# SwiGLU gate and up as a Strassen product of 2x2 blocks, the down product woven between

## The chip, the cores and the metric

One core of one Trainium2 chip runs the whole program. The metric is the device time of one execution in microseconds (us), the median over several executions. The engines are named as the profile names them: PE is TensorE (matrix products, with PEld its weight loads), DVE is VectorE, ACT is ScalarE, POOL is GpSimd, and SP is SyncE, which issues the loads.

## The reference

The program computes a trunk of four layers on 512 frames of width 1024 in float32. Each layer has a mixer (pattern A, B, C, A) and a SwiGLU block; a final RMSNorm ends it.

```python
for i in range(DEPTH):
    hn = rmsnorm(x, norm1_g[i])
    ...
    x = x + y
    x = x + swiglu(rmsnorm(x, norm2_g[i]), ffn_w_gu[i], ffn_w_down[i])
return rmsnorm(x, final_g)

def swiglu(h, w_gu, w_down):
    g, u = jnp.split(h @ w_gu, 2, axis=-1)
    return (jax.nn.silu(g) * u) @ w_down
```

The SwiGLU's inner width is 2816, that is 22 tiles of 128. Only the four SwiGLU blocks are changed.

## The kernel before, in words

Everything is kept with features on the 128 partitions and the 512 frames on the free axis. `X[0..7]` are the eight 128 x 512 tiles of the residual. A float32 operand is split in two parts that TensorE takes at its fast float32r rate: `split` (L125 to L127) makes the high part by a cast on ACT and the low part by a subtraction on DVE. A product of two split operands takes three matmuls, high by high, high by low and low by high (`mm3`, L131 to L133). `dense` (L135) runs `mm3` over the k tiles into one PSUM bank. `weights` (L119) takes a tile of 128 x 1024 weights: it loads 512 KB into `raw` (three buffers) and splits it into `wH` and `wL` (four buffers each).

The norm is applied late. `norm_k` (L226) scales a finished `X[k]` by the norm's weight, and splits it (`hidden_k`, L234: `hH` on ACT at L246, `hL` on DVE at L247), and adds its square to `ssum`. The factor 1/rms per frame comes from `rms_cols` (a column per block of 128 frames, `rcol`) and `rms_rows` (the same along the free axis, `self.r`), and multiplies the products behind the matmuls.

`swiglu` (L301) goes over the 22 inner tiles in groups of 8, 8 and 6. For each tile it takes the gate's weights and the up's weights, each 8 k tiles by 128 outputs, as the stationary operand, with the frames moving, 24 matmuls of 128x512 for each of the two. DVE multiplies both banks by 1/rms (L320, L324), ACT takes the silu (L322), DVE multiplies (L325), and the result is split into `mH`, `mL`. After a group, the down product goes over the 8 output tiles: one tile of weights, 3 matmuls for each inner tile of the group, and `add_x` (L220) adds the bank to `X[m]` on DVE.

Nothing is ordered by a planner: each engine runs its instructions in the order that the tile framework's scheduler gave them when the program was built, and it waits only on semaphores. SP issues all loads, in one order too. A buffer that is taken again makes the instruction that writes it wait for the last reader of what it held.

Of the kernel before, what the change touches and what calls it, by code (L numbers as in the profile page):

```python
# [20 lines left out]
NB = 4  # L21
AH = 16
BH = 8
FT = 22
FGROUPS = ((0, 8), (8, 8), (16, 6))
CW = 2048
CT = 16
EPS = 1e-6
# [3 lines left out]
C_G1, C_G2, C_GF = 0, 32, 64  # L32
# [6 lines left out]
class Trunk:  # L39
# [194 lines left out]
    def hidden_k(self, k):  # L234
        nc = self.nc
        if k == 0:
            self.h_next = []
        g = self.vec[:, self.next_g + k:self.next_g + k + 1]
        if self.next_g == C_GF:
            y = self.hp.tile([P, S], F32, name=self.nm("y"), tag=f"hH{k}")  # L240
            nc.scalar.activation(out=y, in_=self.X[k], func=AF.Identity, scale=g)
            self.h_next.append(y)
        else:
            hi = self.hp.tile([P, S], F32R, name=self.nm("hH"), tag=f"hH{k}")
            lo = self.hp.tile([P, S], F32R, name=self.nm("hL"), tag=f"hL{k}")
            nc.scalar.activation(out=hi, in_=self.X[k], func=AF.Identity, scale=g)  # L246
            nc.vector.scalar_tensor_tensor(out=lo, in0=self.X[k], scalar=g, in1=hi.bitcast(F32),  # L247
                                           op0=ALU.mult, op1=ALU.subtract)
            self.h_next.append((hi, lo))

    def squares_k(self, k, pool=None):

# [45 lines left out]
        return pr  # L298


    def swiglu(self, l):  # L301
        nc = self.nc
        with ExitStack() as es:
            fp = es.enter_context(self.tc.tile_pool(name="ffn", bufs=2, side="right",
                                                    reuse_waits="tile"))
            for k0, kn in FGROUPS:
                acts = []
                for j in range(k0, k0 + kn):
                    gh, gl = self.weights(self.a["w_g"][l, j])
                    pg = self.acc()  # L310
                    self.dense(pg, gh, gl, self.h)
                    if j == 0:
                        self.rms_cols()
                    uh, ul = self.weights(self.a["w_u"][l, j])
                    pu = self.acc()
                    self.dense(pu, uh, ul, self.h)
                    if j == 0:
                        self.rms_rows()
                    g = fp.tile([P, S], F32, name=self.nm("g"), tag="g")
                    nc.vector.tensor_tensor(out=g, in0=pg, in1=self.r, op=ALU.mult)  # L320
                    sg = fp.tile([P, S], F32, name=self.nm("sg"), tag="sg")
                    nc.scalar.activation(out=sg, in_=g, func=AF.Silu)  # L322
                    u = fp.tile([P, S], F32, name=self.nm("u"), tag="u")
                    nc.vector.tensor_tensor(out=u, in0=pu, in1=self.r, op=ALU.mult)  # L324
                    nc.vector.tensor_tensor(out=u, in0=u, in1=sg, op=ALU.mult)  # L325
                    hi, lo = self.part_tiles()
                    self.split(u, hi, lo)
                    acts.append((hi, lo))
                for m in range(KT):
                    dh, dl = self.weights(self.a["w_d"][l, m, :, k0 * P:(k0 + kn) * P], kn * P)  # L330
                    pd = self.acc()
                    self.dense(pd, dh, dl, acts)
                    self.add_x(m, pd, k0 + kn == FT)


    def token_major(self, src, then=None):
# [662 lines left out]
def layouts(i):  # L999

    g = {k: np.asarray(v) for k, v in i.items()}
    c = np.ascontiguousarray

    def stat(w):
        K, M = w.shape
        return c(w.reshape(K // P, P, M // P, P).transpose(2, 1, 0, 3)).reshape(M // P, P, K)
# [9 lines left out]
    def outw(w):  # L1016
        n = w.shape[0] // S
        return c(w.reshape(n, 4, P, 4, 2, P).transpose(0, 3, 2, 4, 1, 5)).reshape(n, 4, P, 1024)

    def cols(v):  # L1020
# [34 lines left out]
        "w_g": np.stack([stat(w[:, :FT * P]) for w in g["ffn_w_gu"]]),  # L1055
        "w_u": np.stack([stat(w[:, FT * P:]) for w in g["ffn_w_gu"]]),
        "w_d": np.stack([stat(w) for w in g["ffn_w_down"]]),
    }


# [14 lines left out]
```

## Time and profile before

| what | value |
|---|---|
| median of 3 runs | 2528.62 us (2526.58 to 2528.68) |
| the profiled execution's own time | 2527.86 us |
| its span, from first to last instruction | 2526.2 us |
| mean granted TensorE clock | 0.996 |
| PE busy | 2498.8 us, 99% |
| DVE busy | 1382.9 us, 55% |
| ACT busy | 1065.9 us, 42% |
| POOL busy | 228.0 us, 9% |
| DMA | 89 GB/s mean over the span |

The share of busy time of PE is that of matmuls that overlap in the pipeline, so how many run one after another is read from their start times. The four SwiGLU blocks lie at about 266 to 630, 901 to 1267, 1544 to 1908 and 2153 to 2509 us of the span.

### The profile page before, as it was taken

How to read it: one execution, taken by the hardware profiler on the slowest of the kernel's cores; microseconds unless marked ns; L12 is line 12 of the kernel's file. 1: busy time of each engine (PE TensorE's matmuls, PEld its weight loads, DVE VectorE, ACT ScalarE, POOL GpSimd, SP SyncE). 2: the span in 40 equal slices, each digit the busy share in tenths (PEclk: the TensorE clock that was granted, in tenths of full speed). 3: DMA queues.
4: the chain of work that ended last, by engine and by line, in shares of the span. 5: the costliest groups of instructions: out<-in, count | busy, mean ns of one | idle time of the engine just before them, and what ended most of it. 6: DMA issues, size and time to landing. Idle time of an engine off the chain costs nothing.

```text
span 2526.2 us, 31856 instructions
## 1 busy us (share of the span) xinstructions
PE 2498.8 (99%) x12156; PEld 2098.5 (83%) x12156; DVE 1382.9 (55%) x2202; ACT 1065.9 (42%) x1779; POOL 228.0 (9%) x369
## 2 busy tenths in 40 slices
PE   8999999999999999999999999999999999999998
PEld 7898888888888888888888888888888888888886
DVE  7777444445777754444537655434456777444443
ACT  7776322223766642222433324222236776322222
POOL 2222100001000110000100001000011222000001
PEclk9999999999999999999999999999999999999998
DMA  4112232323122223232322222323232222232321
GB/s 145 60 60 76 99 93 100 93 95 103 62 76 84 92 92 99 93 101 91 101 92 91 93 84 100 93 99 98 94 93 76 69 68 76 92 98 94 101 88 62
DMA packets 69416, 226.00 MB, mean 89 GB/s; under 512 B 11793, under 2 KB 12817, under 8 KB 69265
## 3 DMA queue, kind: packets, MB, share of 16 engines
q1 hardware_dynamic: 69264, 223.98, 27.2%
q8 instruction: 96, 1.57, 0.3%
q14 instruction: 56, 0.45, 0.1%
HBM read 221.55 MB, written 2.10 MB: 89 GB/s over the span
## 4 chain that ended last, share of the span: by engine, by line
PE 95%; ACT 2%; DVE 2%; issue 1%; POOL 0%; DMA 0%; SPq 0%; DVEq 0%; POOLq 0%; ACTq 0%
PE acc L131 26%; PE acc L133 26%; PE acc L132 26%; PE acc L171 2%; PE acc L173 2%; PE acc L172 2%; PE pt L524 1%; PE acc L350 1%; PE acc L351 1%; PE acc L352 1%; PE po L539 1%; PE s L502 1%; PE s L501 1%; PE po L538 1%; PE ps L927 0%
## 5 line engine op out<-in xcount | busy, mean ns | idle before, releaser
L126 ACT CAST wH<-raw 128x1024 fp32r<-128x1024 f32 (+2 forms) x427 | 438.7, 1028 | 1118.1 <-PE acc L132 969.7
L131 PE MATMUL acc<-hH,wH 128*128 128x512 f32 x1984 | 783.2, 395 | 0.0
L133 PE MATMUL acc<-hH,wL 128*128 128x512 f32 x1984 | 773.9, 390 | 0.0
L132 PE MATMUL acc<-hL,wH 128*128 128x512 f32 x1984 | 773.2, 390 | 0.0
L127 DVE TENSOR_TENSOR wL<-raw,wH 128x1024 fp32r<-128x1024 f32 (+2 forms) x427 | 510.1, 1195 | 118.1 <-ACT wH L126 96.5
L133 PEld LDWEIGHTS acc<-hH,wL 128*128 128x128 f32 x1984 | 372.4, 188 | 78.7
L131 PEld LDWEIGHTS acc<-hH,wH 128*128 128x128 f32 x1984 | 372.8, 188 | 72.8 <-issue 0.5
L132 PEld LDWEIGHTS acc<-hL,wH 128*128 128x128 f32 x1984 | 373.1, 188 | 72.0 <-issue 0.2
L131 PE MATMUL acc<-mH,wH 128*128 128x512 f32 x1024 | 402.2, 394 | 0.2
L132 PE MATMUL acc<-mL,wH 128*128 128x512 f32 x1024 | 399.3, 390 | 0.0
L133 PE MATMUL acc<-mH,wL 128*128 128x512 f32 x1024 | 399.3, 390 | 0.0
L220 DVE TENSOR_TENSOR X<-acc,X 128x512 f32<-128x512 f32 x176 | 121.4, 690 | 281.5 <-PE acc L133 281.3
L133 PEld LDWEIGHTS acc<-mH,wL 128*128 128x128 f32 x1024 | 192.2, 188 | 39.7
L131 PEld LDWEIGHTS acc<-mH,wH 128*128 128x128 f32 x1024 | 192.3, 188 | 39.3 <-ACT mH L126 1.5
L132 PEld LDWEIGHTS acc<-mL,wH 128*128 128x128 f32 x1024 | 192.5, 188 | 38.8 <-DVE mL L127 1.5
L324 DVE TENSOR_TENSOR u<-acc,rbc 128x512 f32<-128x512 f32 x88 | 60.8, 691 | 282.2 <-PE acc L133 282.2
L269 POOL TENSOR_TENSOR ssum<-ssum,sq 128x512 f32<-128x512 f32 x51 | 79.6, 1561 | 1141.3 <-ACT sq L264 1116.9
L320 DVE TENSOR_TENSOR g<-acc,rbc 128x512 f32<-128x512 f32 x88 | 60.8, 691 | 188.1 <-PE acc L133 188.1
L171 PE MATMUL acc<-wH,hH 128*128 128x256 f32 x384 | 116.2, 303 | 6.0 <-ACT hH L246 6.0
L173 PE MATMUL acc<-wH,hL 128*128 128x256 f32 x384 | 110.1, 287 | 1.3 <-DVE hL L247 1.3
L172 PE MATMUL acc<-wL,hH 128*128 128x256 f32 x384 | 109.5, 285 | 0.3 <-DVE wL L127 0.3
L512 POOL TENSOR_SCALAR p<-p,sm 128x128 f32<-128x128 f32 (+3 forms) x128 | 71.6, 560 | 306.8 <-DVE sm L511 298.8
(209 smaller groups left out, 2584.3 us busy)
## 6 DMA issues: line engine op xcount, KB each, us to landing
raw<-in_w_g SPq DMA_DIRECT2D x88, 512.0 KB, 3.2
raw<-in_w_u SPq DMA_DIRECT2D x88, 512.0 KB, 3.2
raw<-in_w_d SPq DMA_DIRECT2D x64, 512.0 KB, 3.5
raw<-in_w_d SPq DMA_DIRECT2D x32, 384.0 KB, 3.2
raw<-in_a_q SPq DMA_DIRECT2D x16, 512.0 KB, 3.4
raw<-in_a_k SPq DMA_DIRECT2D x16, 512.0 KB, 3.4
raw<-in_a_o SPq DMA_DIRECT2D x16, 512.0 KB, 3.3
raw<-in_b_qk SPq DMA_DIRECT2D x16, 512.0 KB, 3.2
```

Of the source, the lines that this page charges most:

```text
L126: self.nc.scalar.copy(out=hi, in_=src)
L127: self.nc.vector.tensor_tensor(out=lo, in0=src, in1=hi.bitcast(F32), op=ALU.subtract)
L131: mm(ps, lH, rH, start=first, stop=False)
L132: mm(ps, lH, rL, start=False, stop=False)
L133: mm(ps, lL, rH, start=False, stop=last)
L171: mm(ps, hh[:, t], wh[:, c], start=k == 0, stop=False)
L172: mm(ps, hh[:, t], wl[:, c], start=False, stop=False)
L173: mm(ps, hl[:, t], wh[:, c], start=False, stop=k == KT - 1)
L220: self.nc.vector.tensor_tensor(out=self.X[m], in0=ps, in1=self.X[m], op=ALU.add)
L269: eng.tensor_tensor(out=t, in0=t, in1=sq, op=ALU.add)
L320: nc.vector.tensor_tensor(out=g, in0=pg, in1=self.r, op=ALU.mult)
L512: nc.gpsimd.tensor_scalar(out=p[:, :n], in0=p[:, :n], scalar1=sm, scalar2=0.0, op0=ALU.mult, op1=ALU.add)
```

## The change

The four SwiGLU blocks are written anew. Of the 22 inner tiles the first two (`FSTD`) are made as before. The other twenty make five chunks (`NCH`) of four tiles, 512 inner features each. For a chunk, gate and up together are one product of frames (512) by model width (1024) by gate and up (2 x 512). It is cut in 2x2 blocks in all three, and made of seven block products instead of eight, each with sums of blocks on either side (a Strassen product in Winograd's form).

- **Operands exchanged.** In a block product the weights move (512 columns at a time) and the frames are stationary: 4 k tiles x 2 blocks of 128 frames x 3 matmuls of 128x512, 24 in all (L402, L404, L405). Its results lie with frames on the partitions.
- **Sums of frames.** Four forms `F[1..4]` of the normed frames (each 512 x 256) are made once per layer by `ffn_forms` and split. For this `hidden_k` writes a third tile `y` per k on ACT (L259).
- **Sums of weights.** The blocks b11, b12, b22, b21 of a chunk are loaded as two tiles of 128x1024 each; `prep` adds them in place on DVE (L384, for four of the seven products) and splits the result. It is called one product ahead.
- **PSUM.** Products 1, 2, 3 and 6 accumulate in two banks `psA`, products 5 and 4 in two banks `psC`, product 7 in two of the four `acc` banks. Between them ACT copies what `psA` holds (L486), DVE subtracts it from `psC` (L489) or adds it to product 7 (L497), and ACT and DVE make silu and product (L492, L493, L498, L499), with 1/rms as a scalar per partition.
- **Turning back.** The chunk's activations are turned to features on partitions by 16 transposes on PE (L434), four to a bank, which are woven into product 5 of the next chunk; each bank is split into `mH`, `mL`.
- **Down product.** `down_steps` makes the 8 output tiles for the four inner tiles of one chunk (or the two of the first part), one tile of weights for two steps (or four). The steps of the chunk before are put between the block products, as many as `FILL` and, in the last chunk, `LAST` say. `add_x` runs 48 times a layer, 24 before.
- **Loads.** The bytes are the same; the weights are laid out in other blocks on the host, and b12 and b21 take turns in the same two buffers.

The core of the diff:

```diff
-FGROUPS = ((0, 8), (8, 8), (16, 6))
+FSTD = 2
+NCH = (FT - FSTD) // 4
+ORDER = (1, 5, 2, 3, 4, 6, 7)
+FILL = (0, 0, 2, 3, 1, 1, 1)
+LAST = (0, 0, 1, 2, 0, 0, 4)
...
     def hidden_k(self, k):
...
             self.h_next.append((hi, lo))
+            if C_G2 <= self.next_g < C_GF:
+                tag = ("mH", "mL")[k % 2]
+                y = self.mp.tile([P, S], F32, name=self.nm("y"), tag=tag)
+                nc.scalar.activation(out=y, in_=self.X[k], func=AF.Identity, scale=g)
+                self.y.append(y)
...
+    def ffn_forms(self, fp, n, F):
...
+                in0, in1, op = {
+                    1: lambda: (y[k][:, B], y[k + 4][:, B], ALU.subtract),
+                    2: lambda: (F["raw", 1, i][:, q], y[k][:, A], ALU.subtract),
+                    3: lambda: (y[k][:, A], y[k][:, B], ALU.subtract),
+                    4: lambda: (y[k + 4][:, A], F["raw", 2, i][:, q], ALU.add)}[n]()
+                nc.vector.tensor_tensor(out=r[:, q], in0=in0, in1=in1, op=op)
+            F["raw", n, i] = r
+            self.split(r, *(t[:, 2 * i:2 * i + 2] for t in F[n]))
+
+    def down_steps(self, src, acts, n, last):
...
+        def step(m):
+            if m % per == 0:
+                st["w"] = self.weights(src[m // per], per * n * P)
+            ps = self.acc()
+            self.dense(ps, *st["w"], acts, m % per * n * P)
+            self.add_x(m, ps, last)
...
     def swiglu(self, l):
...
+                    for i in range(2):
+                        t = fp.tile([P, 1024], F32, name=self.nm("r" + blk),
+                                    tag={"b11": "ra", "b12": "rb", "b21": "rb", "b22": "rc"}[blk])
+                        nc.sync.dma_start(out=t, in_=a["w_s"][l, c, BLOCKS.index(blk), i])
...
+            prods = {1: ("a11", "b11", None), 5: (1, "b11", "b12"), 2: (2, "b11", "b22"),
+                     3: (3, "b12", "b22"), 4: (4, "b22", None), 6: ("a22", "b11", "b21"),
+                     7: ("a12", "b21", None)}
+
+            def prep(p):
...
+                    if more:
+                        nc.vector.tensor_tensor(out=x, in0=x, in1=R[more, i], op=ALU.add)
...
+                    self.split(x, *w)
...
+                def step(k, b):
...
+                    mm(banks[b], xh, wh, start=first and k == 0, stop=False,
+                       skip_group_check=True)
+                    mm(banks[b], xh, wl, start=False, stop=False, skip_group_check=True)
+                    mm(banks[b], xl, wh, start=False, stop=k == 3,
+                       skip_group_check=True)
+                return [lambda k=k, b=b: step(k, b) for k in range(4) for b in range(2)]
...
+                    for b in range(NB):
+                        nc.tensor.transpose(pt[:, b * P:(b + 1) * P], act[b][:, f * P:(f + 1) * P],
+                                            self.ident)
+                    acts.append(self.part_tiles())
+                    self.split(pt, *acts[-1])
...
+            for c in range(NCH):
...
+                for i, p in enumerate(ORDER):
+
+                    q = ORDER[(i + 1) % 7]
+                    if not (last and i == 6):
+                        prep(q)
+                    if q == 3:
+                        load(c, "b21")
...
+                    banks = {1: A, 2: A, 3: A, 6: A, 5: C, 4: C, 7: B}[p]
+                    steps = product(p, banks, p in (1, 5, 7))
+                    if p == 5:
+                        self.weave(steps, turns)
...
+                        if p in (1, 2, 3):
+                            V[p, b] = T(f"v{p}")
+                            nc.scalar.copy(out=V[p, b], in_=A[b])
+                        if p in (3, 4):
+                            v = V[{3: 3, 4: 2}[p], b]
+                            nc.vector.tensor_tensor(out=v, in0=C[b], in1=v, op=ALU.subtract)
...
+                    n = (LAST if last else FILL)[i]
+                    for f in downs[:n]:
+                        f()
```

What this does to the order of the instructions is shown at two places. On PE before, in the middle of a SwiGLU block, the up product of one inner tile ends (`acc_732`) and the gate product of the next begins (`acc_741`):

```order
L131 MATMUL acc_732_3401<-hH_691_3187,wH_730_3396 128x512
L132 MATMUL acc_732_3401<-hL_692_3188,wH_730_3396 128x512
L133 MATMUL acc_732_3401<-hH_691_3187,wL_731_3397 128x512
L131 MATMUL acc_741_3443<-hH_654_3023,wH_739_3438 128x512
L132 MATMUL acc_741_3443<-hL_655_3024,wH_739_3438 128x512
L133 MATMUL acc_741_3443<-hH_654_3023,wL_740_3439 128x512
```

On PE now, in the third chunk of layer 0, the end of product 5 (`psC`), one bank's four transposes (`acc_926`) and the start of product 2 (`psA`, whose frames are the form `F2`):

```order
L402 MATMUL psC_906_4264<-wH_909_4271,F1_725_3321 128x512
L404 MATMUL psC_906_4264<-wL_910_4272,F1_725_3321 128x512
L405 MATMUL psC_906_4264<-wH_909_4271,F1_726_3322 128x512
L434 MATMUL acc_926_4364<-ident_108,v2_853_3957 128x128
L434 MATMUL acc_926_4364<-ident_108,v2_854_3959 128x128
L434 MATMUL acc_926_4364<-ident_108,v3_866_4031 128x128
L434 MATMUL acc_926_4364<-ident_108,v3_867_4034 128x128
L402 MATMUL psA_903_4261<-wH_913_4304,F2_729_3333 128x512
L404 MATMUL psA_903_4261<-wL_914_4305,F2_729_3333 128x512
L405 MATMUL psA_903_4261<-wH_913_4304,F2_730_3334 128x512
```

The matmuls keep their shape of 128x512; the weights are now named first (they move), and the transposes stand among them.

On DVE before, what lies between two inner tiles: the factor for gate and up, their product, and the low parts of weights (`wL`) and activations (`mL`):

```order
L320 TENSOR_TENSOR g_733_3426<-acc_728_3370,rbc_706_3278 128x512
L127 TENSOR_TENSOR wL_753_3512<-raw_751_3510,wH_752_3511 128x1024
L324 TENSOR_TENSOR u_735_3430<-acc_732_3401,rbc_706_3278 128x512
L325 TENSOR_TENSOR u_735_3430<-u_735_3430,sg_734_3428 128x512
L127 TENSOR_TENSOR wL_757_3543<-raw_755_3541,wH_756_3542 128x1024
L127 TENSOR_TENSOR mL_737_3434<-u_735_3430,mH_736_3433 128x512
```

On DVE now, around the end of product 5 and in product 2 of the third chunk: the low parts of product 2's weights (`wL_914`, `wL_916`), of product 3's (`wL_930`, `wL_932`), of the four turned activations (`mL`), a sum of blocks for product 6 (`rb11` with `rb21`), and the low part of the down product's weights (`wL_939`):

```order
L133 TENSOR_TENSOR wL_914_4305<-rb11_881_4101,wH_913_4304 128x1024
L133 TENSOR_TENSOR wL_916_4310<-rb11_882_4103,wH_915_4309 128x1024
L133 TENSOR_TENSOR mL_919_4325<-acc_917_4319,mH_918_4324 128x512
L133 TENSOR_TENSOR wL_930_4375<-rb12_888_4153,wH_929_4374 128x1024
L133 TENSOR_TENSOR mL_922_4340<-acc_920_4334,mH_921_4339 128x512
L133 TENSOR_TENSOR mL_925_4355<-acc_923_4349,mH_924_4354 128x512
L133 TENSOR_TENSOR wL_932_4380<-rb12_889_4155,wH_931_4379 128x1024
L133 TENSOR_TENSOR mL_928_4370<-acc_926_4364,mH_927_4369 128x512
L384 TENSOR_TENSOR rb11_881_4101<-rb11_881_4101,rb21_933_4383 128x1024
L133 TENSOR_TENSOR wL_939_4417<-raw_937_4415,wH_938_4416 128x1024
```

Where a tile's weights took one instruction of 1024 elements for 24 matmuls, a product's weights now take two to four, and the sum that reads the newly loaded `rb21_933` stands ahead of `wL_939`, which the first down step reads.

More of the change, by code (lines that the diff above doesn't have):

```diff
@@ L298, in rms_rows @@
         return pr
+    def ffn_forms(self, fp, n, F):
+        nc, y = self.nc, self.y
+        A, B = slice(0, 256), slice(256, 512)
+        F[n] = tuple(fp.tile([P, 4, 256], F32R, name=self.nm(f"F{n}"), tag=f"F{n}{x}", bufs=1)
+                     for x in "HL")
+        for i in range(2):
+            r = fp.tile([P, 2, 256], F32, name=self.nm("fr"),
+                        tag={1: "v1", 2: "v2", 3: "sg", 4: "v3"}[n])
+            for q in range(2):
+                k = 2 * i + q
+                in0, in1, op = {
[7 more added lines that the diff above has]
+    def down_steps(self, src, acts, n, last):
+        st = {}
+        per = D // (n * P)
+        def step(m):
[4 more added lines that the diff above has]
+            self.add_x(m, ps, last)
+        return [lambda m=m: step(m) for m in range(KT)]
     def swiglu(self, l):
-        nc = self.nc
+        nc, a = self.nc, self.a
+        mm = nc.tensor.matmul
         with ExitStack() as es:
@@ L305, in swiglu @@
                                                     reuse_waits="tile"))
-            for k0, kn in FGROUPS:
-                acts = []
[L308 to L333, printed above, removed]
@@ new lines, in standard @@
+            def standard(j):
+                gh, gl = self.weights(a["w_g"][l, j])
+                pg = self.acc()
+                self.dense(pg, gh, gl, self.h)
+                if j == 0:
+                    self.rms_cols()
+                uh, ul = self.weights(a["w_u"][l, j])
+                pu = self.acc()
+                self.dense(pu, uh, ul, self.h)
+                if j == 0:
+                    self.rms_rows()
+                sg, u = T("sg"), T("v3")
+                nc.vector.tensor_tensor(out=sg, in0=pg, in1=self.r, op=ALU.mult)
+                nc.scalar.activation(out=sg, in_=sg, func=AF.Silu)
+                nc.vector.tensor_tensor(out=u, in0=pu, in1=self.r, op=ALU.mult)
+                nc.vector.tensor_tensor(out=u, in0=u, in1=sg, op=ALU.mult)
+                hi, lo = self.part_tiles()
+                self.split(u, hi, lo)
+                return hi, lo
@@ new lines, in turn, with step @@
+            def turn(act, acts):
+                def step(f):
+                    pt = self.acc()
+                    for b in range(NB):
[3 more added lines that the diff above has]
+                    self.split(pt, *acts[-1])
+                return [lambda f=f: step(f) for f in range(4)]
+            acts = []
+            for j in range(FSTD):
+                acts.append(standard(j))
+                if j == 0:
+                    for blk in ("b11", "b12", "b22"):
+                        load(0, blk)
+                    self.ffn_forms(fp, 1, F)
+                    self.ffn_forms(fp, 2, F)
+                if j == 1:
+                    prep(1)
+                    self.ffn_forms(fp, 3, F)
+                    self.ffn_forms(fp, 4, F)
@@ L336, in token_major @@
+            for f in downs:
+                f()
     def token_major(self, src, then=None):
@@ L1018, in outw, with quads, downw @@
         return c(w.reshape(n, 4, P, 4, 2, P).transpose(0, 3, 2, 4, 1, 5)).reshape(n, 4, P, 1024)
+    def quads(w):
+        w = w.reshape(2, 2, 2, P, 2, FT * P)[..., FSTD * P:].reshape(2, 2, 2, P, 2, NCH, S)
+        return c(w.transpose(5, 0, 4, 1, 3, 2, 6)).reshape(NCH, 4, 2, P, 2 * S)
+    def downw(w):
+        n = w.shape[0] // P
+        per = D // (n * P)
+        t = w.reshape(n, P, KT // per, per, P).transpose(2, 1, 3, 0, 4)
+        return c(t).reshape(KT // per, P, per * n * P)
     def cols(v):
```

75 lines of the change are left out of this document (71 added, 4 removed).

## The prediction

> **What bounds the kernel now.** I read the page first: the busy times, then the chain that ended last.
>
> ```profile
> PE 2498.8 (99%) x12156; PEld 2098.5 (83%) x12156; DVE 1382.9 (55%) x2202; ACT 1065.9 (42%) x1779; POOL 228.0 (9%) x369
> PE 95%; ACT 2%; DVE 2%; issue 1%; POOL 0%; DMA 0%; SPq 0%; DVEq 0%; POOLq 0%; ACTq 0%
> ```
>
> PE is never short of work and makes 95% of the chain. Shares are means over unlike stages, so next come the windows over the four SwiGLU blocks, the only stages that change, and ahead of them one over the first mixer's attention, needed later.
>
> ```profile
> core 0: us, PE busy (x) PEld busy (x) DVE busy (x) ACT busy (x) POOL busy (x), PEclk, DMA share, GB/s
> 100.00:260.00 160.00, 159.89 (x942) 138.58 (x940) 121.98 (x288) 111.71 (x244) 42.90 (x69) 1.00 0.21 69
> 270.00:630.00 360.00, 360.00 (x1628) 299.51 (x1627) 161.09 (x193) 107.64 (x134) 10.07 (x18) 1.00 0.30 96
> 907.00:1267.00 360.00, 360.00 (x1593) 297.99 (x1592) 160.67 (x189) 107.01 (x130) 9.74 (x6) 1.00 0.30 97
> 1550.00:1908.00 358.00, 358.00 (x1617) 297.78 (x1617) 160.89 (x190) 107.35 (x131) 10.69 (x8) 1.00 0.30 96
> 2159.00:2509.00 350.00, 349.75 (x1548) 289.48 (x1546) 148.28 (x175) 101.03 (x123) 7.87 (x6) 1.00 0.28 88
> ```
>
> PE is busy in all of each block at clock 1.00, while DVE works 45% of it (161.09 of 360) and ACT 30%. The waits say the same from the other side: DVE and ACT wait for PE.
>
> ```profile
> ACT wH L126 <- PE acc L132: 969.7, 298, 8.3
> DVE u L324 <- PE acc L133: 282.2, 84, 3.8
> ```
>
> So a SwiGLU block costs what its matmuls cost on PE, one behind another, and the next question is the time from one to the next, read from start times.
>
> ```profile
> 1621.91 0.39 PE L131 MATMUL acc<-hH,wH 128*128 128x512 f32 x1
> ...
> 1627.35 0.39 PE L131 MATMUL acc<-mH,wH 128*128 128x512 f32 x1
> ```
>
> The first begins a bank of 24, the second the next bank: 5.44 us / 24 = 0.2267 us each. A block has 22 x 48 + 22 x 24 = 1584 of them, 1584 x 0.2267 = 359.1 us, which is what the windows hold.
>
> **The change, part by part.** *Matmuls.* In the new block the two standard tiles take 96, the five chunks 5 x 7 x 24 = 840 and the down product 528, together 1464: 120 fewer, 120 x 0.2267 = 27.2 us a block. That needs the exchanged operands (weights moving, frames stationary) to run at the same rate. One mixer product already runs so, three matmuls to each of these rows:
>
> ```profile
> 1300.83 0.39 PE L350 MATMUL acc<-wH,hH 128*128 128x512 f32 x1
> ...
> 1301.51 0.39 PE L350 MATMUL acc<-wH,hH 128*128 128x512 f32 x1
> ```
>
> 0.68 / 3 = 0.227 us, and the stationary side changes two times in three in either form. I take the exchange at nothing.
>
> *Transposes.* Added are 80 a block, in 20 runs of four. Attention has such runs:
>
> ```profile
> 225.96 0.40 PE L133 MATMUL acc<-mH,wL 128*128 128x512 f32 x1
> 226.19 0.60 PE L524 MATMUL pt<-ident,p 128*128 128x128 f32 x4
> 226.55 0.48 PE L131 MATMUL acc<-mH,wH 128*128 128x512 f32 x1
> 226.87 0.39 PE L132 MATMUL acc<-mL,wH 128*128 128x512 f32 x1
> ```
>
> and grouped by line:
>
> ```profile
> L524 PE MATMUL pt<-ident,p 128*128 128x128 f32 x320 | 55.9, 273 | 0.4 <-POOL p L512 0.4
> ```
>
> From 226.19 to 226.87 lie four transposes and one matmul: 0.68 - 0.227 = 0.453 us for the four, 0.113 each. Bounds: by their width against the matmuls, 0.2267 x 128 / 512 = 0.057 each, and the grouped row's own duration, 0.273 each. I take 0.113, since it is a difference of start times in a run of the same four; 20 x 0.453 = 9.06 us a block. The Trainium skill ("TensorE: Matmul & The Clock Gate", Part 4: PE-mode transpose) speaks against the change here: it gives about 275 ns for such a transpose inside a kernel, and says that transposes don't keep the clock gate open. The trace has 273 ns as the duration but 113 ns from start to start, and a clock of 1.00 over the attention window that holds such runs; by the page's figure the 320 would cost 88 us and eat the gain.
>
> *Sum on PE.* 27.2 - 9.06 = 18.15 us a block, 72.6 us in four. Against the profiled execution's 2527.86 us: 2455.3.
>
> *DVE, ACT and loads* are costed at nothing as long as PE covers them, and this cover is thinner than before. A chunk on PE lasts 7 x 5.44 + 1.81 (transposes) + 8 x 2.72 (down steps) = 61.7 us. The durations:
>
> ```profile
> L127 DVE TENSOR_TENSOR wL<-raw,wH 128x1024 fp32r<-128x1024 f32 x391 | 477.7, 1222 | 113.3 <-ACT wH L126 91.6 <-PE acc L294 20.4
> L126 ACT CAST wH<-raw 128x1024 fp32r<-128x1024 f32 x391 | 410.3, 1050 | 1036.0 <-PE acc L132 904.2 <-issue 65.3 <-PE acc L352 51.4
> L220 DVE TENSOR_TENSOR X<-acc,X 128x512 f32<-128x512 f32 x176 | 121.4, 690 | 281.5 <-PE acc L133 281.3
> L126 ACT CAST th<-pt 128x512 fp32r<-128x512 f32 x32 | 18.4, 576 | 10.1 <-PE pt L524 10.1
> L322 ACT ACTIVATE sg<-g 128x512 f32<-128x512 f32 x88 | 55.6, 632 | 1.1
> L247 DVE SCALAR_TENSOR_TENSOR hL<-X,vec,hH 128x512 fp32r<-128x512 f32 x64 | 49.6, 779 | 13.4 <-ACT hH L246 13.3
> ```
>
> DVE per chunk: 14 + 4 low parts and 8 sums of 128x1024, 26 x 1.22 = 31.7; 18 of 512 columns (four turned, four subtractions from `psC`, two additions, eight `add_x`) x 0.69 = 12.4; four products with a scalar x 0.78 = 3.1: 47.2 us, 77%. ACT: 18 casts x 1.05, ten copies and casts of 512 x 0.58, four silus x 0.63: 27 us, 44%. A sum of blocks is not in the trace; the nearest rows are the low part of the same size (1.22) and twice `add_x` (1.38). I take 1.22; the other end adds 0.16 to each. Loads are the same bytes in less time.
>
> Neither engine is full, so order decides. The tight place is the first down step after product 2 (the two DVE pieces and the transposes shown with the change). Count from the start of a chunk's product 1: product 1 ends at 5.44, product 5 with its transposes at 12.69, product 2 at 18.13, and the third matmul of the down step needs `wL_939` at 18.58. DVE starts its series when product 7 of the chunk before ends, one down step earlier, at -2.72. From there to `wL_939` it issues 12 of 1.22 (the last sum for product 5, its two low parts, three sums, four low parts for products 2 and 3, the sum with `rb21_933`, `wL_939`), seven of 0.69 (two additions, `X7`, four turned) and two of 0.78: 14.6 + 4.8 + 1.6 = 21.0, so done at 18.3, 0.3 us ahead of need. Neighbours on DVE overlap a little:
>
> ```profile
> 1628.35 0.69 DVE L325 TENSOR_TENSOR u<-u,sg 128x512 f32<-128x512 f32 x1
> 1628.95 1.22 DVE L127 TENSOR_TENSOR wL<-raw,wH 128x1024 fp32r<-128x1024 f32 x1
> ```
>
> The second starts 0.60 after a start of 0.69, 0.09 saved; over 21 instructions up to 1.9 us. Slack 0.3 to 2.2 us. Inside the series stands one wait that is new: the sum reads `rb21_933`, whose load takes the buffer that `wL_930` has just read. `wL_930` ends at 18.3 - 5.7 = 12.6, DVE reaches the sum at 15.9, and loads of this size take
>
> ```profile
> raw<-in_w_g SPq DMA_DIRECT2D x88, 512.0 KB, 3.2
> raw<-in_w_d SPq DMA_DIRECT2D x64, 512.0 KB, 3.5
> ...
> X<-in_x SPq DMA_DIRECT2D x8, 256.0 KB, 5.8
> ```
>
> 3.2 to 3.5, landing at 15.8 to 16.1: in time, or 0.2 late. Behind the waiting sum on DVE stand `wL_939` (PE's next need) and product 3's successors; behind the load on SP only loads not yet needed.
>
> *Waits left over.* In a layer's first chunk the down steps of the first part have half the matmuls (1.36 us each) against the same split work, and the forms 3 and 4 lie on DVE as well: I find the last of their weight tiles 0.7 us late. The last chunk has its turn and its own down product with less between: up to 0.5. Some 0.2 elsewhere: 1.4 a block, 5.6 in four. The entry of the layer adds the `y` tiles on ACT: by rows of 0.72, 0.72 and 0.62 for `hH`, `y` and the square and half a cast of 1.05, 2.59 us for an output tile that takes PE 2.72 or more; covered.
>
> ```profile
> L246 ACT ACTIVATE hH<-X,vec 128x512 fp32r<-128x512 f32 x64 | 45.9, 722 | 29.4 <-DVE X L220 27.1 <-DMA X<-in_x 1.3
> L264 ACT ACTIVATE sq<-X 128x512 f32<-128x512 f32 x62 | 38.0, 618 | 11.7 <-DVE X L220 11.5
> ```
>
> 2455.3 + 5.6 = 2461. The median before lies 0.8 above the profiled execution, and I leave that small difference out.
>
> **The rivals.** *A: DVE paces the chunks.* If its instructions don't overlap, and sums cost 1.38 (five before `wL_939`, 0.8 us) with semaphore delays on top, each chunk waits 1 to 2 us: 20 chunks, 20 to 40 us, 2481 to 2501. For it: 77% busy, one fixed order. Against it: the slack above, and DVE is idle a quarter of each chunk, so a late chunk doesn't delay the next. Chance 0.09.
>
> *B: transposes cost their duration,* 320 x 0.273 = 87.4 instead of 36.2: 51 us more, 2512. For it: here the weights moving beside them are of another product than in attention. Against it: the start times above. This is where the Trainium skill's 275 ns would lead (same page and section). Chance 0.04.
>
> *C, slower: the load of `rb21` comes late* and holds DVE's queue ahead of `wL_939`. Without overlap the sum must start by 18.58 - 2.44 = 16.1, so a landing time up to 3.5 us is free, with overlap up to 4.9. Each us beyond costs 20 us. It eats 72.6 - 5.6 = 67 us when 20 (t - 3.5) = 67 or 20 (t - 4.9) = 67: from a landing of 6.9 to 8.3 us. The longest row, eight loads issued at once, is 5.8, which gives 18 to 46 us (2479 to 2507). At 8 us without overlap: 2461 + 90 = 2551. For it: several loads are issued close together there, and this one only when SP gets to it. Against it: 512 KB take 3.2 to 3.5 at 96 GB/s, and the same bytes in 5% less time are about 101. Chance 0.05, of it 0.04 slower and 0.01 no change.
>
> *That the change doesn't do what it says* has no chance worth a number: the order shows 1464 matmuls a block.
>
> **How the numbers follow.** The forecast has 0.82; A 0.09; B 0.04; C 0.05. Within 0.2% (5 us, about what a measurement of this kernel can tell from no change) lies only C's 0.01, slower C's other 0.04, all else is faster: 0.95. Low end: no waits (2455.3), and the 1 us a block that the windows hold beyond 359.1 gone too, 2451, say 2450; transposes at 0.057 (18 us less) I leave out, since the run of four speaks against it. High end 2492: the forecast with one more us a chunk and the lower half of A. Outside stay B, half of A, most of C: 0.13.
>
> **What would show it.** The profile after should have PE x11996 (12156 - 480 + 320), SwiGLU blocks of about 343 us, psA and psC matmuls 0.227 apart, runs of four transposes worth 0.45, DVE at three quarters in the blocks, and PE waits there of about 1 to 2 us a block, in the first and last chunks. PE waiting for `wL` after product 2 in every chunk: A if DVE had no gap, C if DVE waited for a DMA at L384. Transposes 0.27 apart: B. Matmuls of the new form further apart than 0.227 would break the first term itself.

## The result, and the profile after

The changed kernel takes 2470.57 us (median; 2469.21 to 2471.75) against 2528.62 us: a ratio of 0.9772, with a 95% interval of 0.9755 to 0.9789. It is 58.1 us faster. Forecast were 2461 us, with a range of 2450 to 2492. The profiled execution's span went from 2526.2 to 2468.5 us, 57.7 less.

The busy times of the page after, and then windows (core 0: us, busy time of PE, PEld, DVE, ACT and POOL, granted clock, share and rate of DMA): layer 0 from its entry to the middle of the first chunk, then the steady chunks of layer 0, then the same two of layer 1.

```profile
PE 2437.8 (99%) x11996; PEld 2042.6 (83%) x11996; DVE 1785.0 (72%) x2626; ACT 1282.5 (52%) x2075; POOL 228.5 (9%) x369
```

```profile
262.00:300.00 38.00, 36.60 (x161) 29.79 (x160) 34.24 (x49) 22.09 (x31) 4.98 (x2) 0.96 0.05 15
300.00:580.00 280.00, 280.00 (x1263) 230.96 (x1263) 205.56 (x221) 121.59 (x147) 1.61 (x20) 1.00 0.31 102
880.00:914.00 34.00, 33.80 (x156) 27.68 (x155) 32.59 (x49) 20.08 (x30) 5.86 (x3) 1.00 0.09 32
914.00:1200.00 286.00, 286.00 (x1291) 236.01 (x1290) 210.34 (x226) 124.96 (x150) 0.00 (x0) 1.00 0.30 100
```

PE has the 11996 instructions that were forecast. In the steady chunks PE is never idle, DVE works 73% of them (205.56 of 280) and ACT 43%; 77% and 44% had been worked out. The entry of the layer is another matter: there DVE is busy 34.24 of 38 us, 90%, and in layer 1 96%. No window over a whole block shows that.

A run of four transposes with its neighbours, and the first run of the chunk after, on PE of the changed kernel (start, duration, instruction):

```profile
405.90 0.60 PE L434 MATMUL acc<-ident,v 128*128 128x128 f32 x4
406.26 0.48 PE L402 MATMUL psC<-wH,F 128*128 128x512 f32 x1
406.58 0.40 PE L404 MATMUL psC<-wL,F 128*128 128x512 f32 x1
...
467.76 0.60 PE L434 MATMUL acc<-ident,v 128*128 128x128 f32 x4
```

From 405.90 to 406.58 are 0.68 us, less one matmul of 0.227: 0.453 for the four, as in attention. A chunk takes 467.76 - 405.90 = 61.86 us; 61.7 was worked out.

Where the 57.7 us lie shows when the span is cut at the first matmul with `ssum` of every norm between a mixer and a SwiGLU block, read from PE's rows (the last 17 us, the final norm, are left out):

| stretch | before | after | difference |
|---|---|---|---|
| start to block 0 | 265.67 | 267.86 | +2.2 |
| block 0 | 364.22 | 349.44 | -14.8 |
| mixer 1 | 270.65 | 271.23 | +0.6 |
| block 1 | 366.50 | 349.90 | -16.6 |
| mixer 2 | 276.88 | 277.68 | +0.8 |
| block 2 | 364.22 | 347.74 | -16.5 |
| mixer 3 | 244.74 | 246.55 | +1.8 |
| block 3 | 355.59 | 340.94 | -14.7 |

Worked out were 18.15 us a block, 72.6 together, less 5.6 of waits. The blocks gave 62.5, and 5.4 were lost in the mixers, which the change does not touch but for their end, where the next norm is made. That end, layer 0, on PE of the changed kernel, with what the wait was for in brackets:

```profile
265.34 0.39 PE L137 MATMUL acc<-hH,wH 128*128 128x512 f32 x1
266.93 0.50 PE L138 MATMUL acc<-hL,wH 128*128 128x512 f32 x1 [1.20 <-DVE hL L253]
267.26 0.40 PE L139 MATMUL acc<-hH,wL 128*128 128x512 f32 x1
267.86 1.07 PE L293 MATMUL acc<-ones,ssum 128*128 128x1 f32 x8 [0.20 <-DVE ssum L280]
268.80 0.78 PE L137 MATMUL acc<-hH,wH 128*128 128x512 f32 x1
269.37 0.63 PE L138 MATMUL acc<-hL,wH 128*128 128x512 f32 x1
...
271.93 0.51 PE L138 MATMUL acc<-hL,wH 128*128 128x512 f32 x1
272.28 0.40 PE L139 MATMUL acc<-hH,wL 128*128 128x512 f32 x1
```

In the kernel before, the same stretch (three matmuls and the eight of `ssum`) lies between these two rows:

```profile
264.99 0.39 PE L131 MATMUL acc<-hH,wH 128*128 128x512 f32 x1
...
266.47 0.48 PE L131 MATMUL acc<-hH,wH 128*128 128x512 f32 x1
```

It took 1.48 us and now takes 3.46 (265.34 to 268.80), 2.0 more. Two things are new in it and behind it. PE waits 1.36 us beyond the pitch for the last `hL` and some 0.4 for `ssum`. And behind these waits the matmuls start 0.43 us apart instead of 0.227 until 272.28. The windows over 260 to 268 and 268 to 272 us say why, for the changed kernel and, below, for the one before:

```profile
260.00:268.00 8.00, 6.60 (x30) 4.85 (x28) 7.96 (x13) 5.40 (x10) 1.87 (x2) 1.00 0.19 66
268.00:272.00 4.00, 4.00 (x16) 3.32 (x17) 4.00 (x7) 2.27 (x3) 1.37 (x1) 0.60 0.12 23
```

```profile
260.00:268.00 8.00, 8.00 (x41) 6.78 (x40) 4.48 (x6) 3.24 (x4) 2.21 (x2) 1.00 0.19 66
268.00:272.00 4.00, 4.00 (x19) 3.31 (x18) 0.00 (x0) 0.02 (x1) 2.33 (x21) 1.00 0.39 131
```

The granted clock fell to a mean of 0.60 behind a PE that was idle 1.4 of 8 us. DVE, busy 4.48 us in the window before, is busy 7.96 in it now. What it does there is in its rows:

```profile
256.33 1.49 DVE L337 TENSOR_TENSOR fr<-y,y 128x256 f32<-128x256 f32 x1
257.86 0.42 DVE L337 TENSOR_TENSOR fr<-fr,y 128x256 f32<-128x256 f32 x1
258.20 1.22 DVE L133 TENSOR_TENSOR wL<-raw,wH 128x1024 fp32r<-128x1024 f32 x1
259.33 1.78 DVE L253 SCALAR_TENSOR_TENSOR hL<-X,vec,hH 128x512 fp32r<-128x512 f32 x1
...
263.78 1.49 DVE L337 TENSOR_TENSOR fr<-y,y 128x256 f32<-128x256 f32 x1
265.19 0.68 DVE L133 TENSOR_TENSOR F<-fr,F 128x512 fp32r<-128x512 f32 x1
265.80 0.41 DVE L337 TENSOR_TENSOR fr<-fr,y 128x256 f32<-128x256 f32 x1
266.13 0.74 DVE L253 SCALAR_TENSOR_TENSOR hL<-X,vec,hH 128x512 fp32r<-128x512 f32 x1
```

The forms (L337, and the low part `F`) are made as soon as their `y` are there, between the residual's tiles, and so ahead of the last `hL` at 266.13 that PE waits for. Some take 1.49 us where the same shape takes 0.42, and one `hL` 1.78 where the last takes 0.74. That is when GpSimd adds squares:

```profile
256.25 1.29 POOL L280 TENSOR_TENSOR ssum<-ssum,sq 128x512 f32<-128x512 f32 x1 [1.41 <-ACT sq L275]
258.94 1.62 POOL L280 TENSOR_TENSOR ssum<-ssum,sq 128x512 f32<-128x512 f32 x1 [1.40 <-ACT sq L275]
263.69 1.30 POOL L280 TENSOR_TENSOR ssum<-ssum,sq 128x512 f32<-128x512 f32 x1 [3.12 <-ACT sq L275]
```

Each long DVE instruction begins beside one of these and ends 0.3 to 0.6 us behind its end.

### The profile page after: what moved, and what is told of

Its sections match the earlier page's. It is cut to its first block, busy times and chain, and to the rows that moved or that the text cites. A ratio compares the mean times of both kernels' runs of the same rounds, so it can differ in the third digit from the quotient of the medians.

```text
span 2468.5 us, 32002 instructions
## 1 busy us (share of the span) xinstructions
PE 2437.8 (99%) x11996; PEld 2042.6 (83%) x11996; DVE 1785.0 (72%) x2626; ACT 1282.5 (52%) x2075; POOL 228.5 (9%) x369
## 4 chain that ended last, share of the span: by engine, by line
PE 90%; DVE 5%; ACT 3%; issue 1%; POOL 0%; DMA 0%; SPq 0%; DVEq 0%; POOLq 0%; ACTq 0%
PE acc L137 14%; PE acc L139 14%; PE acc L138 14%; PE psA L402 6%; PE psA L404 6%; PE psA L405 6%; PE psC L402 3%; PE psC L404 3%; PE psC L405 3%; PE acc L177 2%; PE acc L179 2%; PE acc L178 2%; PE acc L402 1%; PE acc L405 1%; PE acc L404 1%; PE pt L705 1%
## 5 line engine op out<-in xcount | busy, mean ns | idle before, releaser
L132 ACT CAST wH<-rb 128x1024 fp32r<-128x1024 f32 x280 | 293.2, 1050 | 499.9 <-PE acc L138 154.8
L133 DVE TENSOR_TENSOR wL<-rb,wH 128x1024 fp32r<-128x1024 f32 x280 | 339.1, 1221 | 151.9 <-ACT wH L132 143.7
L132 ACT CAST wH<-raw 128x1024 fp32r<-128x1024 f32 (+1 forms) x259 | 268.6, 1038 | 295.3 <-PE acc L138 135.8
L133 DVE TENSOR_TENSOR wL<-raw,wH 128x1024 fp32r<-128x1024 f32 (+1 forms) x259 | 314.7, 1215 | 137.8 <-ACT wH L132 136.8
L139 PE MATMUL acc<-mH,wL 128*128 128x512 f32 x1024 | 399.9, 390 | 0.0
L137 PE MATMUL acc<-hH,wH 128*128 128x512 f32 x704 | 286.9, 408 | 0.0
L138 PE MATMUL acc<-hL,wH 128*128 128x512 f32 x704 | 276.9, 393 | 2.6 <-DVE hL L253 2.6
L139 PE MATMUL acc<-hH,wL 128*128 128x512 f32 x704 | 277.1, 394 | 0.0
L139 PEld LDWEIGHTS acc<-mH,wL 128*128 128x128 f32 x1024 | 192.2, 188 | 41.5 <-DVE wL L133 1.2
L384 DVE TENSOR_TENSOR rb<-rb,rb 128x1024 f32<-128x1024 f32 x160 | 192.4, 1219 | 6.8 <-DMA rb<-in_w_s 5.6
L139 PEld LDWEIGHTS acc<-hH,wL 128*128 128x128 f32 x704 | 132.9, 189 | 29.1
L138 PEld LDWEIGHTS acc<-hL,wH 128*128 128x128 f32 x704 | 133.7, 190 | 26.3 <-DVE hL L253 4.3
L137 PEld LDWEIGHTS acc<-hH,wH 128*128 128x128 f32 x704 | 133.3, 189 | 23.3 <-issue 0.5
L402 PE MATMUL psC<-wH,F 128*128 128x512 f32 x320 | 129.7, 405 | 0.0
L402 PE MATMUL psA<-wH,F 128*128 128x512 f32 x320 | 127.0, 397 | 0.0
L404 PE MATMUL psC<-wL,F 128*128 128x512 f32 x320 | 125.7, 393 | 0.0
```

What stands on the lines that cost most here:

```text
L132: self.nc.scalar.copy(out=hi, in_=src)
L133: self.nc.vector.tensor_tensor(out=lo, in0=src, in1=hi.bitcast(F32), op=ALU.subtract)
L137: mm(ps, lH, rH, start=first, stop=False)
L138: mm(ps, lH, rL, start=False, stop=False)
L139: mm(ps, lL, rH, start=False, stop=last)
L384: nc.vector.tensor_tensor(out=x, in0=x, in1=R[more, i], op=ALU.add)
```

## The experiments

The theory after the result: the gain is the count of matmuls, less 0.113 us a transpose, as worked out; what fell short of it was lost at the layer's entry, to the forms on DVE. The rivals: transposes cost more, DVE paces the chunks, or ACT's third tile makes the norm late. Times are medians; each set has its own runs of the kernel before on the same chip (2526.85, 2528.70, 2528.53 and 2527.80 us), so a ratio is the fairer number.

**Without the transposes.** The split takes the chunk's activations as they stand.

```diff
-                    pt = self.acc()
-                    for b in range(NB):
-                        nc.tensor.transpose(pt[:, b * P:(b + 1) * P], ...
-                    self.split(pt, *acts[-1])
+                    self.split(act[f], *acts[-1])
```

> Leaves out the 320 transposes: each turned tile is split from the chunk's activations as they stand, frames on partitions, so what the down product reads is another tensor. Theory (a transpose costs what the start times show, 0.113 us each, 0.453 us a run of four): 320 x 0.113 = 36 us below the changed kernel, 2470.6 - 36 = 2434 us. Rival (a transpose costs its duration, 0.272 us): 87 us below, 2484 being out of reach and 2383 us the value.

Measured: 2433.66 us, ratio 0.9628 (0.9614 to 0.9642). Against the changed kernel's 0.9772 that is 0.0144 of 2528 us, 36.4 us for 320 transposes or 0.114 each. Rival B of the prediction, by which they cost their duration of 0.272, is out.

**Without the forms.** No `y`, no `ffn_forms`, and the four products that read a form read blocks of the frames.

```diff
-            if C_G2 <= self.next_g < C_GF:
+            if False:
...
-                if src in (1, 2, 3, 4):
-                    return [t[:, k, b * P:(b + 1) * P] for t in F[src]]
+                src = {1: "a11", 2: "a12", 3: "a21", 4: "a22"}.get(src, src)
```

> Leaves out the forms F[1..4] and the tiles y: the products that read forms read blocks of the normed frames instead, with the same number and shape of matmuls. Theory (of the 15 us between the 72.6 us worked out and the 57.6 us that came, most is lost at the entry of the layer, where the forms on VectorE delay the last hL and PE then runs at half rate for 3.4 us in two layers): the four mixers become 5.4 us shorter up to the matmuls of ssum, and the half-rate stretches of about 3.3 us go too, together 8 to 9 us: 2462 us, granted clock 1.00 throughout the entry. Rival (the loss is spread over the chunks, in VectorE's order and the matmuls' pace): 2468 to 2471 us, with the entry still late because ACT still has nothing to do with it.

Measured: 2459.25 us, ratio 0.9730 (0.9714 to 0.9746), a span of 2457.4. The windows of layer 0's entry:

```profile
260.00:268.00 8.00, 8.00 (x41) 6.79 (x40) 4.47 (x7) 3.53 (x5) 1.84 (x2) 1.00 0.21 76
268.00:272.00 4.00, 4.00 (x20) 3.30 (x19) 3.02 (x3) 0.00 (x0) 2.47 (x5) 1.00 0.00 0
```

PE has no idle time and the clock is 1.00. The mixers are back at 266.27, 270.64, 276.88 and 244.76 us, 4.8 less than in the changed kernel. Of 11.1 us of span the theory had 8 to 9; the rest is in the chunks, which take 61.72 us here instead of 61.86 (below).

**`y` without the forms.** The same, but ACT still makes the `y` tiles.

> As the run without forms, but the tiles y are still made on ACT and nothing reads them. Theory (VectorE's form instructions, not ACT's y, hold up the last hL): within 1.5 us of the run without forms, 2462 us. Rival (ACT's third tile per output makes hH, and with it hL, late): as the changed kernel at the entry, 2469 to 2471 us.

Measured: 2459.70 us, ratio 0.9732 (0.9717 to 0.9746), a span of 2457.4 again. ACT's third tile costs nothing; the cause is the making of the forms on DVE or the products' use of them, which a run below takes apart.

**Without the sums of weights.** `prep` leaves out L384.

```diff
-                    if more:
+                    if False:
```

> Leaves out the eight sums of weight blocks in every chunk (the products take plain blocks), 8 x 1.22 = 9.8 us less on VectorE in each of 20 chunks. Theory (VectorE's work in the chunks lies wholly beside PE's): no difference beyond 2 us, 2469 to 2471 us; chunks still 61.8 us. Rival (VectorE paces the chunks a little, which is why a chunk takes 61.85 and not 61.7 us): 3 us or more below, 2467 us or less, with chunks of 61.7 us.

Measured: 2471.03 us, ratio 0.9776 (0.9762 to 0.9791), chunks of 61.85 us. In the window from 300 to 580 us DVE's busy time falls from 205.56 to 167.84 us, and nothing follows. DVE does not pace the steady chunks: rival A is out there.

**The forms behind `ssum`.** The order is changed and nothing is left out: forms 1 and 2 may issue only after the last addition to `ssum`.

```diff
-        eng.tensor_tensor(out=t, in0=t, in1=sq, op=ALU.add)
+        self.sum_ins = eng.tensor_tensor(out=t, in0=t, in1=sq, op=ALU.add)
...
-                    self.ffn_forms(fp, 1, F)
-                    self.ffn_forms(fp, 2, F)
+                    with self.tc.issue_after(self.sum_ins.ins):
+                        self.ffn_forms(fp, 1, F)
+                        self.ffn_forms(fp, 2, F)
```

> The forms 1 and 2 may issue only after the last addition to ssum; nothing is left out. Theory (at the layer's entry VectorE does forms ahead of the last hL, which stops PE for up to 2 us and, in layers 0 and 3, puts it at half rate for 3.4 us): the entry is as before the change, 4 to 5 us of waits and 3 us of half rate go, 2462 to 2464 us, clock 1.00 at the entry of all four blocks. Rival (the work is only pushed back and makes the first chunk late instead): 2468 us or more.

Measured: 2467.60 us, ratio 0.9762 (0.9747 to 0.9776): some 3 us below the changed kernel, which is less than half of the theory's gain, within the intervals of the two ratios, and nearer to the rival. The entry is mended (265.67 us to block 0, as before the change), but a few microseconds on, PE (first row) waits for GpSimd's 1/rms (second row):

```profile
273.58 1.16 PE L305 MATMUL acc<-ident,rcol 128*128 128x128 f32 x8 [1.40 <-POOL rcol L299]
```

```profile
267.03 6.49 POOL L299 TENSOR_TENSOR rcol<-ms,mhalf 128x4 f32<-128x4 f32 x1 [4.18 <-DVE ms L296]
```

At this place in the kernel before, GpSimd's row is

```profile
266.89 1.95 POOL L288 TENSOR_TENSOR rcol<-ms,mhalf 128x4 f32<-128x4 f32 x1 [5.79 <-DVE ms L285]
```

What took 1.95 us takes 6.49 while DVE runs through the forms, their low parts and, of weights, a low part and two sums. The wait has been moved.

**The forms made and not read.** Only the products' operand is changed (as in the run without forms).

> The forms are made as in the changed kernel, but the products read blocks of the normed frames in their place; what it leaves out is their use. Theory (of the 11.3 us that leaving out forms and their use saved, about 8 were the entry and about 2.8 came from chunks that took 61.72 instead of 61.86 us): the entry stays late, chunks take 61.72 us, 2467 to 2468 us. Rival (the chunks' 0.14 us have nothing to do with the operand): 2470 to 2471 us with chunks of 61.86 us.

Measured: 2465.53 us, ratio 0.9753 (0.9738 to 0.9767): 2 us below what was expected. The entry stays late, and the steady chunks take 61.72 us:

```profile
406.36 0.60 PE L433 MATMUL acc<-ident,v 128*128 128x128 f32 x4
...
468.09 0.60 PE L433 MATMUL acc<-ident,v 128*128 128x128 f32 x4
```

So 0.13 us a chunk, 2.6 us in 20, come from the form as the stationary operand, apart from its making. The 2 us below the expectation are no third cost of the forms: in this execution the clock did not fall behind the wait at layer 3's entry, worth 1.6 us (last section), and the final norm was 1.5 us shorter.

**One sum twice.** The sum of `rb11` with `rb21` ahead of `wL_939` is issued twice.

```diff
+                      for _ in range(1 + (p == 6 and i == 0)):
                         nc.vector.tensor_tensor(out=x, in0=x, in1=R[more, i], op=ALU.add)
```

> One sum of each chunk, the one of rb11 with rb21 that stands ahead of the first down step's low part, is done twice, 1.22 us more on VectorE in the tight series (the products of a doubled sum are another number). Theory (slack of 0.3 to 2.2 us at that place, as worked out before): a wait of 0 to 0.9 us in each of 20 chunks, 2471 to 2489 us. Rival (the cover is far thicker than worked out): 2470 to 2472 us, no wait there.

Measured: 2470.57 us, ratio 0.9776 (0.9759 to 0.9792): no difference in the median, as the rival had it. The trace is finer: in each layer the third and fourth chunks take 62.07 to 62.11 us, and the four blocks lose some 2.7 us by it. The span hides that (2468.5 us again), because in this execution the clock did not fall at layer 3's entry, worth 1.6 us, and the final norm was 0.9 us shorter. The 0.2 us more stand where they were expected, in the first down step after product 2, where three starts are 0.23, 0.33 and 0.34 apart:

```profile
479.12 0.40 PE L138 MATMUL acc<-mL,wH 128*128 128x512 f32 x1
479.35 0.40 PE L137 MATMUL acc<-mH,wH 128*128 128x512 f32 x1
479.68 0.50 PE L139 MATMUL acc<-mH,wL 128*128 128x512 f32 x1
480.02 0.40 PE L137 MATMUL acc<-mH,wH 128*128 128x512 f32 x1
```

1.22 us more on DVE cost 0.2. The matmul that reads the low part (L139) also stands one place later here than in the changed kernel, 0.23 us, so the slack in the changed kernel's own order is about 0.8 us. In the changed kernel itself the low part ends at 417.06 and its product begins at 417.30, with the third matmul, which reads it, at 417.76, 0.7 us behind; DVE and PE:

```profile
414.43 1.21 DVE L384 TENSOR_TENSOR rb<-rb,rb 128x1024 f32<-128x1024 f32 x1
415.83 1.23 DVE L133 TENSOR_TENSOR wL<-raw,wH 128x1024 fp32r<-128x1024 f32 x1 [0.19 <-ACT wH L132]
```

```profile
417.30 0.39 PE L137 MATMUL acc<-mH,wH 128*128 128x512 f32 x1
417.52 0.40 PE L138 MATMUL acc<-mL,wH 128*128 128x512 f32 x1
417.76 0.39 PE L139 MATMUL acc<-mH,wL 128*128 128x512 f32 x1
```

**All sums twice.** As above, for all eight (`range(2)`).

> All eight sums of a chunk are done twice, 9.8 us more on VectorE, 57 of 61.7 us (the doubled sums are another number). Theory (the order, not the share, sets the cover: five of the eight stand in the series ahead of the first down step's low part, 6.1 us against a slack of 0.3 to 2.2): PE waits 2 to 5.8 us in a chunk, 40 to 115 us in 20, 2510 to 2585 us. Rival (VectorE at 92% still fits): under 2480 us.

Measured: 2496.94 us, ratio 0.9876 (0.9861 to 0.9891): 26 us more, between the two. Steady chunks take 62.8 to 63.0 us, 1.0 more, and from a layer's first chunk to its second it is 3 to 5 us more. The theory sized it wrongly, since the scheduler did not keep the order. All ten sums do stand ahead of `wL_939` on DVE; but on PE 14 matmuls of product 3 now stand ahead of the first down step, so its low part is needed later, and the waits are in product 3 and in the next down step (0.4 and 0.6 us). In that order DVE has room for nearly all of 9.8 us in a chunk; in the changed kernel's order it was not tested.

**The forms behind 1/rms.** As with `ssum`, but `issue_after` the first product with 1/rms (L421 of the first inner tile).

> The forms 1 and 2 may issue only after the first product with 1/rms of the layer's first inner tile; nothing is left out. Theory (the run with the forms behind the last ssum freed the entry, and then lost 1.5 us a block because VectorE's instructions with two operands in SBUF drew GpSimd's 1/rms out to up to 6.49 us and PE waited for it): with the forms behind 1/rms both waits go and the clock stays at 1.00; the 0.14 us a chunk stays: 2470.6 - 4.8 - 3.3 = 2462.5 us. Rival (the forms then come too late for the first chunk): 2466 us or more, with PE waiting for F in product 5.

Measured: 2469.14 us, ratio 0.9765 (0.9752 to 0.9779), no gain clear of the intervals. The rival's time came, in a place a little ahead of the one it named. Block 0 starts at 265.62 us and GpSimd's 1/rms takes 1.95 us again; but in every block PE now waits in the first chunk, at the second half of product 5, for weights whose sum stands on DVE behind forms 3 and 4:

```profile
291.95 0.63 PE L402 MATMUL psC<-wH,F 128*128 128x512 f32 x2
293.75 0.50 PE L402 MATMUL psA<-wH,F 128*128 128x512 f32 x1 [1.18 <-ACT wH L132]
```

Product 5 began at 289.20, so 291.95 is its middle: two matmuls (0.45), then 1.35 us of wait. (A few records are missing around it in the trace, and `psA` in the second row is a name out of place.) With what follows some 1.8 us a block are lost.

**Forms that are copies.** The same instructions and buffers, with the maximum of a block with itself for the sum.

> The forms are plain copies of blocks of the normed frames (a maximum of a block with itself) and not sums; as many instructions, in the same buffers. It is read for the time of a chunk alone. Theory A (the place of F in SBUF costs the 0.14 us a chunk): 61.85 us. Theory B (its numbers do): 61.72 us.

Read for the chunk alone, in a single run: 467.40 - 405.55 = 61.85 us, theory A:

```profile
405.55 0.60 PE L435 MATMUL acc<-ident,v 128*128 128x128 f32 x4
...
467.40 0.60 PE L435 MATMUL acc<-ident,v 128*128 128x128 f32 x4
```

It is not the numbers in `F` that cost 0.13 us a chunk. What of the tile does (its place in SBUF or its layout of 4 x 256) was not taken apart.

**`rb21` loaded twice.** The second load into the same buffer follows the first.

```diff
-                        nc.sync.dma_start(out=t, in_=a["w_s"][l, c, BLOCKS.index(blk), i])
+                        for _ in range(1 + (blk == "b21")):
+                            nc.sync.dma_start(out=t, in_=a["w_s"][l, c, BLOCKS.index(blk), i])
```

> Each load of rb21 is made twice into the same buffer, the second after the first, so that the sum with it waits for about twice 3.3 us. Theory (rival C's price: landing is free up to 3.5 to 4.9 us, each us beyond costs 20 us): 6.6 us of landing give 34 to 62 us, 2505 to 2533 us. Rival (there is more slack than the walk shows, as in the run with doubled sums): under 2490 us.

Measured: 2477.05 us (2469.96 to 2477.51), ratio 0.9788 (0.9773 to 0.9804). Of the 6.5 us more, some 4.5 lie in the layers' first chunks: there DVE waits 1.3 to 2.9 us for the second load, ahead of a low part of down weights, and PE 0.5 to 1.8 us for that low part. About 3 are two more stretches of 3.4 us at half clock, one behind the entry of layer 0 and one in the next mixer; the final norm was 0.9 us shorter. Steady chunks stay at 61.85 us, so there the run does not test the price that rival C was given: the scheduler put the sum behind `wL_939`, and nothing of PE's stood behind the wait any more. What a late load costs in the changed kernel's own order stays open; that no such wait came in it is seen from its steady chunks.

**Forms 3 and 4 later.** As the run with the forms behind 1/rms, and `ffn_forms` 3 and 4 are called in the first chunk, behind `prep` of product 2.

```diff
                     if not (last and i == 6):
                         prep(q)
+                    if c == 0 and i == 1:
+                        self.ffn_forms(fp, 3, F)
+                        self.ffn_forms(fp, 4, F)
```

> As the run with forms 1 and 2 behind 1/rms, and forms 3 and 4 are asked for only after the weights of product 2; nothing is left out. Theory (from the layer's entry to the middle of the first chunk VectorE is full, at 90 to 96%, so a form done there delays whatever stands behind it, and a form is free only where its own reader is the next that is late; forms 3 and 4 are read last): the 1.8 us a block that PE lost inside product 5 go, 2461 to 2463 us. Rival (VectorE is so full that the wait moves on once more, to product 3): 2467 to 2470 us, with PE waiting for wL in product 3.

Measured: 2465.60 us (2464.90 to 2466.54), ratio 0.9753 (0.9740 to 0.9767): the best of the kernels that leave nothing out, some 5 us below the changed kernel, whose own runs were all above 2469. The intervals of the two ratios overlap, so the size is uncertain. It came between theory and rival: the waits at the entry and in product 5 are gone, and a smaller one has come, at the start of product 3, for ACT's copy of `psA`; PE:

```profile
299.60 0.39 PE L405 MATMUL psA<-wH,F 128*128 128x512 f32 x1
300.76 0.50 PE L402 MATMUL psA<-wH,F 128*128 128x512 f32 x1 [0.78 <-ACT v L488]
```

and ACT, whose copies stand behind a cast that waited 2.93 us for a sum on DVE:

```profile
299.18 1.05 ACT L132 CAST wH<-rb 128x1024 fp32r<-128x1024 f32 x1 [2.93 <-DVE rb L384]
300.13 1.06 ACT L488 COPY v<-psA 128x512 f32<-128x512 f32 x2
```

About 1 us a block is left there, and DVE is still behind it.

## Why the prediction was right, and where it was not

- **What bounds, and the first term (120 matmuls a block, 27.2 us): right.** Without the forms, the span fell by 2526.2 - 2457.4 = 68.8 of the 72.6 us worked out. In that run the mixers are as before, and 3.8 us are missing over four blocks; some 1.2 of them are the last chunk's 16 transposes, which run by themselves (2.0 us instead of 1.81, with 0.1 at the next start). The rest I did not place.
- **Transposes at 0.113 us: right,** by the start times after and by the run without them (0.114). The figure that the Trainium skill gives ("TensorE: Matmul & The Clock Gate", Part 4: PE-mode transpose; measured there with bf16), about 275 ns, is the duration here as well (272 ns), and not what a transpose costs in a run of four; and the clock stayed at 1.00 in the chunks that hold them. "Eat the gain" was too strong for that figure: rival B's own time, 2512 us, is still below 2528.
- **The exchanged operands at nothing: nearly right.** Products that read the frames keep the pitch; those that read forms add 0.13 us a chunk, 2.6 us in all. No row of before had a form in it.
- **DVE and ACT covered in the steady chunks: right.** `wL_939` was worked out to end 0.3 to 2.2 us ahead of its need; it ends 0.7 ahead, and a sum added there cost 0.2 of its 1.22 us, with the reader 0.23 us later.
- **The waits left over, 5.6 us in the first and last chunks: wrong in place.** Those chunks lost some tenths. PE waited somewhere else.
- **The step that failed is "The entry of the layer ... covered".** It counted ACT's `y` alone, and ACT did have the room (the run with `y` and without forms). It left out that forms 1 and 2 depend on nothing but `y`, so that DVE makes them between the residual's tiles, ahead of the last `hL`. In the span this cost 4.8 us of waits at four entries and, from two of these, 3.2 us at half clock (the starts between 268.80 and 272.28 in layer 0 are 1.6 us further apart than the pitch allows, in layer 3 as much). With the forms' 2.6 us in the chunks that makes 10.6 of the 11.1 us that leaving them out gave back.
- **The rivals:** B and A (in the steady chunks) are out. A held at a place that it didn't name: DVE is full at 90 to 96% from the entry to the middle of the first chunk, and three attempts to move the forms there each brought a new wait. C didn't occur; its price could not be tested in the order that was priced, but in the first chunks a load made later did hold DVE and, behind it, PE.
- The total came 9.6 us above the forecast, 9.3 of it in the span: 11.1 of forms and 3.8 of small losses, less the 5.6 that had been set aside for other waits. It lay within the range, but by luck: the room above the forecast had been left for waits in the chunks, which did not come, and it covered a loss at the entry that had been put at nothing.

## What to carry to other kernels

A change that lightens the engine at the bound is worth its count of instructions only where the others keep up, so work out their share for each stage, and the short stage at which a new tensor is first made above all: 73% in the steady chunks said nothing of 90 to 96% at the entry. List everything that can start as soon as its inputs are there, since a scheduler will put it ahead of what the bound engine needs next; and when such work is moved, ask what is late next, because on a full engine the wait moves with it. An idle microsecond or two of PE can cost as much again in clock.

## What the runs showed of the hardware

- **A short wait can bring the clock down, and does not always.** From 265.34 to 268.80 in layer 0 PE takes 2.0 us longer than before the change, in layer 3 as much, and the matmuls that followed ran 0.43 us apart for some 3.4 us. In layers 1 and 2, with waits of 0.13 and 0.33 us at `hL` and the same 0.4 at `ssum`, the clock stayed at 1.00. The long wait, of 1.36 to 1.40 us at `hL`, stands at 14 entries in the traces of seven kernels (the changed one and the runs without transposes, without sums, with unread forms, with one and with all sums twice, and with `rb21` loaded twice). Behind nine of them the clock fell; behind five it did not, as in layer 3 with unread forms (1.00 over 2110 to 2117 us, against 0.76 in the changed kernel). What else decides it is not shown here. The Trainium skill ("TensorE: Matmul & The Clock Gate", Part 1: The HAM clock gate) gives half speed after an idle window of about 3.4 us, and full speed after a busy one of that length. The length of the slow stretch agrees with it; that PE must be idle for a whole window does not, since it was not.
- **DVE and GpSimd hold each other up.** A form of 128x256 takes 0.41 us by itself and 1.49 beside GpSimd's addition of squares; GpSimd's 1/rms of 128x4 takes 1.95 us before, 3.68 in the changed kernel's layer 0 and 6.49 with the forms packed behind `ssum`. Of the 12 forms that lie beside such an addition in the changed kernel 10 take 0.92 to 1.49 us, and the other 52 forms 0.41 or 0.42. The rows that were held up have both inputs in SBUF; `add_x`, with one input in PSUM, takes 0.67 to 0.69 us beside GpSimd too (45 places). So says the Trainium skill ("SBUF — State Buffer", Who interferes with whom): a DVE instruction with two SBUF inputs contends with a GpSimd instruction that reads SBUF.

```profile
270.63 3.68 POOL L299 TENSOR_TENSOR rcol<-ms,mhalf 128x4 f32<-128x4 f32 x1 [5.64 <-DVE ms L296]
```

- **A stationary operand's tile can matter at the third digit:** 61.85 us a chunk with forms as the stationary operand, whatever their numbers, and 61.72 with the frames.
